# A hybrid attention and SSM layer on one core: the capped decay differences and the first conv tap on ScalarE

## The chip, the cores and the metric

The kernel runs on one core of a Trainium2 chip. The metric is the device time of one execution in microseconds. Before the change it is 1166.08 us, the median of three runs (1162.01, 1166.08 and 1166.91).

## What is computed

One layer of a decoder trunk over 1024 tokens of width 1024, in float32. The input is normalised and modulated, one input projection of 6672 columns feeds a stick-breaking attention group and a Mamba-2 SSM group of 16 heads, and both outputs go through one output projection and a final norm. The change lies in the SSM branch, of which the reference reads, cut to what matters:

```
xbc = silu(causal_depthwise_conv(xbc, conv_w, conv_b))      # 4 taps per channel and a bias
xs, b_ssm, c_ssm = split(xbc)                               # 1024 + 256 + 256 channels
log_decay = dt * a                                          # per token and head
a_cum = cumsum(log_decay within a chunk of 128)             # falls, since a < 0
seg = a_cum[l] - a_cum[s]
decay = exp(where(s <= l, seg, -inf))
y_diag = einsum(cb * decay, xdt)                            # cb = C . B in the chunk
y_off  = einsum(C, state before the chunk, exp(a_cum))
y = y_diag + y_off + x * d_skip
```

The kernel holds a chunk's matrix with s on the partitions and l along the row. It caps seg at 0 before the exponential, so that nothing overflows where s > l, and the mask comes in with cb.

## The kernel before

TensorE does every projection as three float32r matmuls (high x high, low x high, high x low part of both operands), 24 of 128x512 for one tile of 128 columns and half of the tokens (`mm_f`, L265 to L270). A projection tile needs weights loaded by SyncE, a rounded copy `whi` and the rest `wlo` (`split`, L180), and the two PSUM banks of the pool `pj` take turns. Before the pinned part of the program `whi` is made on ScalarE and `wlo` on GpSimd.

The program has three stretches. First the modulation and the first projections, up to about 100 us. Then, to about 360 us, the SSM stretch that the change touches: `conv_tile` (L494) projects one tile of 128 channels, copies it out of PSUM on ScalarE (`conv_in`, L476) into a row `om`, and `conv_post` (L484) does the four taps on VectorE, a Tanh on ScalarE and a last product on VectorE. Twelve tiles go this way: two of C, two of B, eight of x. `ssd_group(g)` (L575) does the scan for eight heads, in eight chunks of 128 tokens. L1003 weaves group 0 with the conv tiles of group 1, L1004 weaves group 1 with four gate tiles (`gate_ssm`) and the first query and key tiles (`qk`). The third stretch, from L1007 (`pinned[0] = True`), is attention with the remaining projections and the output projections, in written program order on every engine.

In the SSM stretch nothing is pinned: the order of each engine's queue is made by a scheduler when the program is built, from its own idea of each instruction's cost. What is issued on an engine runs in that order, and an instruction whose input isn't ready holds all that stand behind it.

A chunk of `ssd_group` runs as follows. ScalarE's queue issues a transfer (L584) that brings the eight heads' a_cum rows, spread to all partitions, into `abc`, half of a tile `be`; the pool has four such tiles, so a chunk's transfer waits until the chunk four before it has let go of its tile. VectorE makes the capped differences `m` in the other half, one 128x128 instruction per head (L585 to L587). ScalarE takes the exponential of `m` and of `abc` (L588, L589). VectorE copies the chunk's last decays to `cdy` (L591). TensorE makes B.C and the transpose of B into `pt` (L594, L595), VectorE copies both out into `cbm` (L597, L598) and multiplies `m` by it (L599). TensorE transposes the x tiles into `pz` (L603), VectorE multiplies by dt into `xd`, a buffer of `v` or `sq` (L605), GpSimd scales `abc` by C (L609). Then come TensorE's sixteen matmuls of the chunk (L614, L619), VectorE's four sums into the x tiles (L622), and the new state: a product on GpSimd (L625), a matmul (L628) and two VectorE instructions into `st` (L634, L635).

All calls on VectorE, ScalarE, GpSimd and SyncE pass through a helper, so the profile gives L62 as their line; they are told apart by the tiles they write and read. `x8` behind a row means eight such instructions in a row.

Of the kernel before, what the change touches and what calls it, by code (L numbers as in the profile page):

```python
# [10 lines left out]
AF = mybir.ActivationFunctionType  # L11
ALU = mybir.AluOpType
# [3 lines left out]
S = 1024  # L16
# [10 lines left out]
def hybrid_layer_kernel(  # L27
# [22 lines left out]
    def K(ins):  # L50

        return tc.keep_in_program_order(ins) if pinned[0] else ins
# [11 lines left out]
    V, A, G, SP = Engine(nc.vector), Engine(nc.scalar), Engine(nc.gpsimd), Engine(nc.sync)  # L64
# [14 lines left out]
    def mk(pool, tag, shape, dtype=F32, bufs=None):  # L79
        uid[0] += 1  # L80
        kw = {} if bufs is None else {"bufs": bufs}
        return pool.tile(shape, dtype, tag=tag, name=f"{tag}_{uid[0]}", **kw)

    def const(name, shape, dtype=F32):
        return cp.tile(shape, dtype, tag=name, name=name)
# [4 lines left out]
    def duo(dtype=F32):  # L90
        return mk(sp, "be", [P, 2, S], dtype, bufs=4)

    def bank(pool, tag):
        return mk(pool, tag, [P, HALF])
# [379 lines left out]
    tri, trigt, acT, dtb, dcol, cw, aneg = late_consts()  # L474
# [4 lines left out]
    def conv_buf():  # L479
        u = mk(sp, "om", [P, 1028], bufs=2)  # L480
        G.memset(u[:, 0:3], 0.0)
        return u

    def conv_post(j, u, dst):  # L484
        V.tensor_scalar(dst, u[:, 3:3 + S], cw[:, 36 + j:37 + j], cw[:, 48 + j:49 + j],
                        op0=ALU.mult, op1=ALU.add)
        for tap in range(2, -1, -1):
            V.scalar_tensor_tensor(dst, u[:, tap:tap + S], cw[:, 12 * tap + j:12 * tap + j + 1],
                                   dst, op0=ALU.mult, op1=ALU.add)
        th = mk(sp, "th", [P, S], bufs=1)  # L490
        A.activation(th, dst, AF.Tanh)
        V.scalar_tensor_tensor(dst, th, 1.0, dst, op0=ALU.add, op1=ALU.mult)

    def conv_tile(j, dst):  # L494
        box = []

        def evac(b, ps):
            if b == 0:
                box.append(conv_buf())
            conv_in(box[0], b, ps)  # L500

        yield from inproj_f(C_XBC + j * P, evac)
        conv_post(j, box[0], dst)
# [9 lines left out]
    for j, ps, dst in ((10, ps_c, Cg[0]), (8, ps_b, Bg[0])):  # L513
        u = conv_buf()
        for b in range(2):
            conv_in(u, b, ps[b])
        conv_post(j, u, dst)
# [47 lines left out]
    acum = const("acum", [P, TB, 16])  # L565
# [9 lines left out]
    def ssd_group(g):  # L575
        Ct, Bt = Cg[g], Bg[g]
        st = None
        hs = slice(8 * g, 8 * g + 8)
        for ch in range(TB):
            ts_ = slice(ch * P, (ch + 1) * P)  # L580
            am = duo().rearrange("p u (h t) -> p u h t", t=P)
            abc, m = am[:, 0], am[:, 1]
            r0 = ch * 16 + 8 * g
            A.dma_start(abc, acT_d[r0:r0 + 8, :].unsqueeze(0).broadcast_to([P, 8, P]))  # L584
            for h in range(8):  # L585
                V.tensor_scalar(m[:, h, :], abc[:, h, :], acum[:, ch, 8 * g + h:8 * g + h + 1], 0.0,
                                op0=ALU.subtract, op1=ALU.min)  # L587
            A.activation(m, m, AF.Exp)  # L588
            A.activation(abc, abc, AF.Exp)  # L589
            cd = mk(sp, "cdy", [P, 8], bufs=2)  # L590
            V.tensor_copy(cd, abc[:, :, P - 1])  # L591

            pc = bank(pt, "pt")
            K(T.matmul(pc[:, 0:P], Bt[:, ts_], Ct[:, ts_], start=True, stop=True))  # L594
            K(T.transpose(pc[:, P:2 * P], Bt[:, ts_], ident))  # L595
            cbm = mk(sp, "cbm", [P, 2, P], bufs=2)
            V.tensor_tensor(cbm[:, 0, :], pc[:, 0:P], tri, op=ALU.mult)  # L597
            V.tensor_copy(cbm[:, 1, :], pc[:, P:2 * P])  # L598
            V.tensor_tensor(m, m, cbm[:, 0:1, :].broadcast_to([P, 8, P]), op=ALU.mult)  # L599

            px = bank(pz, "pz")
            for j in range(4):
                K(T.transpose(px[:, j * P:(j + 1) * P], xs[4 * g + j][:, ts_], ident))  # L603
            xd = mk(sp, "sq" if ch % 2 else "v", [P, 2, 8, 64], bufs=2 if ch % 2 else 3)
            V.tensor_tensor(xd[:, 0], px.rearrange("p (h r) -> p h r", r=64),  # L605
                            dt_t[:, ch, hs].unsqueeze(2).broadcast_to([P, 8, 64]), op=ALU.mult)
            py = bank(pz, "pz")
            if ch > 0:
                G.tensor_tensor(abc, abc, Ct[:, ts_].unsqueeze(1).broadcast_to([P, 8, P]), op=ALU.mult)  # L609
            for j in range(4):  # L610
                for e in range(2):
                    h = 2 * j + e
                    po = py[64 * e:64 * e + 64, j * P:(j + 1) * P]
                    K(T.matmul(po, xd[:, 0, h, :], m[:, h, :], start=True, stop=(ch == 0)))  # L614
                if ch > 0:
                    for e in range(2):
                        h = 2 * j + e
                        po = py[64 * e:64 * e + 64, j * P:(j + 1) * P]
                        K(T.matmul(po, st[:, h, :], abc[:, h, :], start=False, stop=True))  # L619
            for j in range(4):  # L620
                jj = 4 * g + j
                V.scalar_tensor_tensor(xs[jj][:, ts_], xs[jj][:, ts_], dcol[:, jj:jj + 1],  # L622
                                       py[:, j * P:(j + 1) * P], op0=ALU.mult, op1=ALU.add)
            if ch < TB - 1:
                G.tensor_tensor(xd[:, 1], xd[:, 0],  # L625
                                dte[:, ch, hs].unsqueeze(2).broadcast_to([P, 8, 64]), op=ALU.mult)
                pst = bank(pv, "pv")
                K(T.matmul(pst, cbm[:, 1, :], xd[:, 1].rearrange("p h r -> p (h r)"), start=True, stop=True))  # L628
                nst = mk(sp, "st", [P, 8, 64], bufs=2)
                psv = pst.rearrange("p (h r) -> p h r", r=64)  # L630
                if ch == 0:
                    V.tensor_copy(nst, psv)
                else:
                    V.tensor_tensor(nst, st, cd.unsqueeze(2).broadcast_to([P, 8, 64]), op=ALU.mult)  # L634
                    V.tensor_tensor(nst, nst, psv, op=ALU.add)  # L635
                st = nst
            yield 3.4
# [363 lines left out]
    pieces += [("y", i, g, y_d) for i in range(TB) for g in range(2)]  # L1001

    weave((ssd_group(0), 27.0), (chain(bc_tiles(1), xs_tiles(range(4, 8))), 62.0))  # L1003
    weave((ssd_group(1), 27.0), (chain(*[gate_ssm(j) for j in range(4)], qk(0, box)), 63.0))  # L1004
    load_upto(2)
    ahead(), ahead()
# [117 lines left out]
    for i in range(TB):  # L1124
# [27 lines left out]
        for n, (c0, c1) in enumerate(cuts):  # L1152
            ps = bank(pj, "pj")
            for k in range(KT):
                yh, yl = yt[k // 4]
                ks = slice(k % 4 * P, (k % 4 + 1) * P)
                for m, (y, w) in enumerate(((yh, wa_h[k]), (yh, wa_l[k]), (yl, wa_h[k]))):
# [5 lines left out]
                                   op0=ALU.mult, op1=ALU.mult)  # L1163
# [42 lines left out]
```

## Time and profile before

| | |
|---|---|
| median of three runs | 1166.08 us |
| profiled execution, its own time | 1164.38 us |
| its span, first to last instruction | 1162.5 us |
| mean granted TensorE clock | 0.981 of full |
| TensorE busy | 1091.7 us, 94% |
| VectorE busy | 791.7 us, 68% |
| ScalarE busy | 445.6 us, 38% |
| GpSimd busy | 354.7 us, 31% |

A row of a group gives the engine, the operation, what it writes and reads by tile name, the shapes, the count, the busy time in us and the mean of one in ns, and the idle time just before it with what ended it. A row of the waits reads "engine line waited for: us in total, times, longest". Matmuls are pipelined: each is shown longer than the distance to the next one, so the distance of their starts tells the rate.

### The profile page before, as it was taken

To read this page: it belongs to the slowest core of one execution; us is meant where nothing else is said; L and a number is where in the kernel's file an instruction comes from. 1 tells how busy PE (TensorE), PEld (TensorE's weight loads), DVE (VectorE), ACT (ScalarE), POOL (GpSimd) and SP (SyncE) were. 2 spreads that over 40 slices of the span, in tenths; PEclk is the share of its full clock that TensorE was granted. 3 is DMA by queue.
4 is the path that set the end of the run, shared out by engine and by line. 5 is a ranking of instruction groups with operands and counts; after the bars stand their busy time and mean duration, and the time that the engine had idled before them with its cause. 6 is when DMAs were issued, how large, how long until landed. Compare 5 with 4: busy or idle time off the path is not lost. (4 is left out here: it accounts for less than half of the span.)

```text
span 1162.5 us, 16503 instructions
## 1 busy us (share of the span) xinstructions
PE 1091.7 (94%) x6401; PEld 854.3 (73%) x6401; DVE 791.7 (68%) x1292; ACT 445.6 (38%) x942; POOL 354.7 (31%) x245
## 2 busy tenths in 40 slices
PE   5999999898999988999999999999999979999997
PEld 4688877676787766778767787677787747778886
DVE  4566989998975854572697845967549678673444
ACT  4432423332222442444444645445545434350101
POOL 2322445435672343120221202212122134344220
PEclk9999999998999999999999999999999979999999
DMA  9802422122221121110231102111011413375331
GB/s 292 219 20 55 120 55 82 55 73 75 89 66 35 55 73 55 28 55 10 74 91 56 54 19 65 55 28 56 19 37 50 163 42 104 106 259 184 130 133 73
DMA packets 101473, 96.16 MB, mean 83 GB/s; under 512 B 5670, under 2 KB 87826, under 8 KB 101396
## 3 DMA queue, kind: packets, MB, share of 16 engines
q1 hardware_dynamic: 98724, 86.61, 24.7%
q10 hardware_dynamic: 2448, 8.46, 2.2%
q8 instruction: 50, 0.82, 0.3%
q14 instruction: 27, 0.22, 0.1%
q0 software_dynamic: 224, 0.06, 0.0%
HBM read 78.26 MB, written 16.84 MB: 82 GB/s over the span
## 5 line engine op out<-in xcount | busy, mean ns | idle before, releaser
L62 POOL TENSOR_TENSOR wlo<-raw,whi 128x512 fp32r<-128x512 f32 (+1 forms) x113 | 164.2, 1455 | 404.7 <-DVE whi L62 200.0
L269 PE MATMUL pj<-hh,whi 128*128 128x512 f32 x576 | 242.5, 421 | 12.8 <-DVE be L62 5.7
L269 PE MATMUL pj<-hl,whi 128*128 128x512 f32 x576 | 229.7, 399 | 0.0
L269 PE MATMUL pj<-hh,wlo 128*128 128x512 f32 x576 | 229.2, 398 | 0.0
L62 ACT COPY be<-pt 128x512 f32<-128x512 f32 (+3 forms) x190 | 91.2, 480 | 181.2 <-PE pt L823 180.5
L269 PEld LDWEIGHTS pj<-hh,whi 128*128 128x128 f32 x576 | 109.8, 191 | 43.1 <-DVE be L62 7.0
L269 PEld LDWEIGHTS pj<-hh,wlo 128*128 128x128 f32 x576 | 109.5, 190 | 26.3 <-issue 1.0
L269 PEld LDWEIGHTS pj<-hl,whi 128*128 128x128 f32 x576 | 110.0, 191 | 19.5 <-issue 1.1
L823 PE MATMUL pt<-ident,be 128*128 128x128 f32 x569 | 97.7, 281 | 12.8 <-ACT be L62 12.3
L823 PEld LDWEIGHTS pt<-ident,be 128*128 128x128 f32 x569 | 68.2, 142 | 47.9 <-ACT be L62 36.4
L62 DVE TENSOR_TENSOR_SCAN om<-om,ident 128x128 f32<-128x128 f32 x64 | 40.7, 637 | 88.9 <-ACT om L62 88.9
L62 ACT ACTIVATE be<-pz 128x512 f32<-128x512 f32 (+3 forms) x192 | 100.5, 524 | 0.0
L62 DVE TENSOR_TENSOR_SCAN bc<-bc 128x896 f32<-128x896 f32 (+6 forms) x56 | 85.3, 1523 | 2.0
L62 DVE TENSOR_TENSOR_SCAN om<-om 128x896 f32<-128x896 f32 (+6 forms) x56 | 78.4, 1401 | 2.0
L62 ACT ACTIVATE om<-pz 128x512 f32<-128x512 f32 (+2 forms) x96 | 47.6, 495 | 78.8 <-PE pz L768 77.4
L62 POOL TENSOR_TENSOR sq<-sq,th 128x512 f32<-128x512 f32 (+1 forms) x18 | 36.4, 2021 | 114.6 <-ACT th L62 114.6
L835 PE MATMUL pv<-be,v 128*64 128x256 f32 (+1 forms) x640 | 70.4, 365 | 0.0
L311 PE MATMUL pj<-whi,hh 128*128 128x256 f32 (+1 forms) x224 | 67.1, 300 | 0.9 <-ACT om L62 0.9
L768 PE MATMUL pz<-big,big 64*128 64x384 f32 (+2 forms) x576 | 65.2, 357 | 0.2 <-DVE big L62 0.2
L835 PEld LDWEIGHTS pv<-be,v 128*64 128x64 f32 x640 | 43.5, 137 | 29.6 <-issue 9.3
L313 PE MATMUL pj<-whi,hl 128*128 128x256 f32 (+1 forms) x224 | 64.0, 286 | 0.0
L312 PE MATMUL pj<-wlo,hh 128*128 128x256 f32 (+1 forms) x224 | 63.9, 285 | 0.0
(276 smaller groups left out, 2165.4 us busy)
## 6 DMA issues: line engine op xcount, KB each, us to landing
raw<-in_w_in_dram SPq DMA_DIRECT2D x102, 256.0 KB, 2.9
be<-acT_d ACTq DMA_DIRECT2D x16, 512.0 KB, 3.7
big<-in_x_dram SPq DMA_DIRECT2D x11, 512.0 KB, 6.0
aw<-in_w_ada_dram SPq DMA_DIRECT2D x16, 256.0 KB, 5.4
u_d<-big SPq DMA_DIRECT2D x8, 512.0 KB, 3.4
y_d<-bc SPq DMA_DIRECT2D x8, 512.0 KB, 2.6
raw<-in_w_ada_dram SPq DMA_DIRECT2D x16, 256.0 KB, 2.7
raw<-u_d SPq DMA_DIRECT2D x16, 256.0 KB, 3.0
```

The costliest lines, as they stand in the source:

```text
L62: return lambda *args, **kw: K(op(*args, **kw))
L269: K(T.matmul(ps, w[:, ws], h[:, b * HALF:(b + 1) * HALF], start=(k == 0 and n == 0), stop=(k == KT - 1 and n == 2)))
L311: K(T.matmul(ps[:, :n], h_hi[k][:, ts_], whi[:, ws], start=(k == 0), stop=False))
L312: K(T.matmul(ps[:, :n], h_hi[k][:, ts_], wlo[:, ws], start=False, stop=False))
L313: K(T.matmul(ps[:, :n], h_lo[k][:, ts_], whi[:, ws], start=False, stop=(k == KT - 1)))
L768: K(T.matmul(zs[e][:, :mw], a[r, i * P:(i + 1) * P], k_[r, c0:c0 + mw], start=(n == 0), stop=(n == 2)))
L823: K(T.transpose(ptt[:, (j - j0) * P:(j - j0 + 1) * P], be[:, j * P:(j + 1) * P], ident))
L835: K(T.matmul(pav[p][64 * e:64 * e + 64, (q0 + u) * P:(q0 + 2) * P], vs[p][:, j * P + 64 * e:j * P + 64 * e + 64], tl[e][:, u:2, j * P:(j + ...
```

## The change

The first conv tap with the bias goes from a VectorE instruction to a ScalarE ACTIVATE (Identity, with a scale and a bias per partition). The capped difference min(abc - acum, 0) is written as -max(acum - abc, 0): eight ScalarE ACTIVATEs per chunk (Relu, scale -1, acum as bias) give the positive value, and the exponential behind them takes scale -1.

```
 def conv_post(j, u, dst):
-    V.tensor_scalar(dst, u[:, 3:3 + S], cw[:, 36 + j:37 + j], cw[:, 48 + j:49 + j],
-                    op0=ALU.mult, op1=ALU.add)
+    A.activation(dst, u[:, 3:3 + S], AF.Identity, scale=cw[:, 36 + j:37 + j], bias=cw[:, 48 + j:49 + j])
...
         for h in range(8):
-            V.tensor_scalar(m[:, h, :], abc[:, h, :], acum[:, ch, 8 * g + h:8 * g + h + 1], 0.0,
-                            op0=ALU.subtract, op1=ALU.min)
-        A.activation(m, m, AF.Exp)
+            A.activation(m[:, h, :], abc[:, h, :], AF.Relu, scale=-1.0,
+                         bias=acum[:, ch, 8 * g + h:8 * g + h + 1])
+        A.activation(m, m, AF.Exp, scale=-1.0)
```

That is 12 + 128 instructions. Since the scheduler orders the stretch anew, the queues change around them as well. Two places are shown; numbers behind a name tell its buffers apart in the program.

VectorE, group 0, the end of its chunk 3 (counted from 0), before. `v_1724` is the product xd of chunk 4, `big_1585` an x tile of group 1 in its conv taps, `be_1924` the tile of chunk 6, and the four rows with `dcol` are the sums of chunk 3:

```order
L62 TENSOR_SCALAR be_1924<-be_1924,acum 128x128 x8
L62 COPY cdy_1821<-be_1809 128x8
L62 TENSOR_SCALAR big_1585<-om_1679,cw 128x1024
L62 SCALAR_TENSOR_TENSOR big_1585<-om_1679,cw,big_1585 128x1024 x2
L62 SCALAR_TENSOR_TENSOR big_982<-big_982,dcol,pz_1633 128x128
L62 SCALAR_TENSOR_TENSOR big_1056<-big_1056,dcol,pz_1633 128x128
L62 SCALAR_TENSOR_TENSOR big_1130<-big_1130,dcol,pz_1633 128x128
L62 SCALAR_TENSOR_TENSOR big_1204<-big_1204,dcol,pz_1633 128x128
L62 SCALAR_TENSOR_TENSOR big_1585<-om_1679,cw,big_1585 128x1024
L62 TENSOR_TENSOR st_1658<-st_1658,pv_1656 128x512
L62 TENSOR_TENSOR v_1724<-pz_1719,dt_t 128x512
```

The same place on VectorE in the changed program:

```order
L62 COPY cdy_1821<-be_1809 128x8
L62 SCALAR_TENSOR_TENSOR big_1585<-th_1768,big_1585 128x1024
L62 SCALAR_TENSOR_TENSOR big_982<-big_982,dcol,pz_1633 128x128
L62 SCALAR_TENSOR_TENSOR big_1056<-big_1056,dcol,pz_1633 128x128
L62 SCALAR_TENSOR_TENSOR big_1130<-big_1130,dcol,pz_1633 128x128
L62 SCALAR_TENSOR_TENSOR big_1204<-big_1204,dcol,pz_1633 128x128
L62 TENSOR_TENSOR st_1658<-st_1658,pv_1656 128x512
L62 TENSOR_TENSOR v_1724<-pz_1719,dt_t 128x512
```

The nine TENSOR_SCALAR are gone, the taps of `big_1585` have moved ahead of this place, and its last product, which needs ScalarE's Tanh `th_1768`, has moved up to stand before the sums.

ScalarE, group 0, from the transfer of chunk 7 (`be_2020`) to that of the next chunk, before. `om` and `pj` are a projection tile being copied out, `whi` and `raw` weights:

```order
L62 DMA be_2020<-acT_d 128x1024
L62 COPY om_1865<-pj_1784 128x512
L62 ACTIVATE th_1768<-big_1585 128x1024
L62 CAST whi_2086<-raw_2082 128x512
L62 ACTIVATE be_2020<-be_2020 128x1024 x2
L62 CAST whi_2090<-raw_2084 128x512
L62 COPY om_1865<-pj_1868 128x512
L62 DMA be_2155<-acT_d 128x1024
```

The same stretch of ScalarE's queue in the changed program:

```order
L62 DMA be_2020<-acT_d 128x1024
L62 ACTIVATE be_2020<-be_2020,acum 128x128 x8
L62 CAST whi_2090<-raw_2084 128x512
L62 COPY om_1865<-pj_1868 128x512
L62 ACTIVATE be_2020<-be_2020 128x1024 x2
L62 ACTIVATE big_1771<-om_1865,cw 128x1024
L62 DMA be_2155<-acT_d 128x1024
```

The eight Relus stand right behind the transfer that they read, a copy out of `pj` behind them, and the first tap of the next conv tile behind the exponentials.

## The prediction

> **What bounds the kernel now.** I read the page first, then the windows of 50 us, then who waited for whom in the stretch that the change touches. The page says that TensorE is the engine that fills the span:
>
> ```profile
> PE 1091.7 (94%) x6401; PEld 854.3 (73%) x6401; DVE 791.7 (68%) x1292; ACT 445.6 (38%) x942; POOL 354.7 (31%) x245
> ```
>
> The profiled execution took 1164.38 us with a span of 1162.5 us, so 1.9 us lie around it; the median of the three runs is 1166.08 us, 1.7 us above it. The sum below is made as a difference against the profiled execution and then taken from the median.
>
> The changed lines run between about 100 and 360 us, while the chunks of the SSM scan are woven into projections. The third column below is TensorE's busy time, then weight loads, VectorE, ScalarE and GpSimd; after them the granted clock.
>
> ```profile
> 200.00:250.00 50.00, 42.45 (x266) 33.74 (x265) 49.82 (x86) 14.73 (x20) 20.28 (x13) 0.93 0.21 63
> 250.00:300.00 50.00, 44.77 (x244) 34.46 (x243) 43.30 (x78) 17.10 (x23) 25.74 (x15) 0.93 0.27 85
> 300.00:350.00 50.00, 47.42 (x298) 37.45 (x297) 41.57 (x70) 12.08 (x17) 33.34 (x18) 0.97 0.24 74
> ```
>
> ```profile
> 100.00:360.00 260.00, 240.54 (x1379) 189.31 (x1377) 227.51 (x391) 79.91 (x109) 123.64 (x74) 0.97 0.25 74
> ```
>
> VectorE is busy 49.8 of 50 us in the worst of them and 227.5 of 260 in all; ScalarE only 79.9 of 260. TensorE idles 260 - 240.5 = 19.5 us. Its waits there, in the view of waits (total, times, longest), say for whom:
>
> ```profile
> PE pz L614 <- DVE v L62: 5.9, 4, 2.5
> PE pz L603 <- DVE big L62: 3.8, 3, 3.4
> PE pz L614 <- DVE sq L62: 2.9, 2, 2.6
> PE pt L594 <- DVE cbm L62: 2.7, 2, 1.7
> PE pj L269 <- DVE th L62: 2.1, 1, 2.1
> PE pj L269 <- ACT om L62: 1.6, 1, 1.6
> PE pv L628 <- POOL sq L62: 0.4, 1, 0.4
> ```
>
> They add up to 19.4 us, 17.4 of them behind VectorE. So in this stage, and not in the rest of the kernel, VectorE's queue sets the pace.
>
> A wait costs more than itself, because the matmuls after it run slowly for a while:
>
> ```profile
> 319.67 0.72 PE L269 MATMUL pj<-hh,whi 128*128 128x512 f32 x1 [2.14 <-DVE th L62]
> 320.19 0.63 PE L269 MATMUL pj<-hl,whi 128*128 128x512 f32 x1
> ...
> 323.30 0.39 PE L269 MATMUL pj<-hh,whi 128*128 128x512 f32 x1
> 323.53 0.39 PE L269 MATMUL pj<-hl,whi 128*128 128x512 f32 x1
> ```
>
> At full clock one projection matmul follows another after 0.23 us; after the wait of 2.14 us the first spacing is 0.52. The granted clock of the three windows gives the size: 50 x (0.07 + 0.07 + 0.03) = 8.5 us. All that this stage could give back is therefore 19.4 + 8.5 = 28 us. The Trainium skill (TensorE: Matmul & The Clock Gate, Part 1: The HAM clock gate) puts the drop after at least one idle window of about 3.4 us; the trace shows it after 2.14 us, so the measurement decides. By the page alone only the one wait of 3.4 us would cost clock, nearly all of the clock term below would fall out, and the time would be about 1155 us.
>
> **What the change takes from VectorE.** 128 capped differences and the first taps (twelve in all, eight of them in the second row):
>
> ```profile
> L62 DVE TENSOR_SCALAR be<-be,acum 128x128 f32<-128x128 f32 x128 | 46.2, 427 | 2.9 <-DMA be<-acT_d 2.9
> ...
> L62 DVE TENSOR_SCALAR big<-om,cw 128x1024 f32<-128x1024 f32 x8 | 7.4, 928 | 2.7 <-ACT om L62 2.6
> ```
>
> ```profile
> L62 DVE TENSOR_SCALAR be<-be,acum x128: 270/274/2447, 121.9 to 318.7; 128x128 f32<-128x128 f32 x128
> ```
>
> That is 46.2 + 7.4 = 53.6 us. The median of 274 ns against a mean of 427 says that some of it is waiting inside the instruction, which may move to its neighbours: 128 x 0.274 + 7.4 = 42.5 us is the lower bound. VectorE falls from 227.5 to between 174 and 185 us of 260, 67 to 71%.
>
> How this reaches TensorE is seen at one wait. VectorE's time line (start, length), and TensorE's:
>
> ```profile
> 194.94 3.46 DVE L62 TENSOR_SCALAR be<-be,acum 128x128 f32<-128x128 f32 x8
> ...
> 198.40 0.80 DVE L62 TENSOR_SCALAR big<-om,cw 128x1024 f32<-128x1024 f32 x1
> ...
> 206.62 0.68 DVE L62 TENSOR_TENSOR v<-pz,dt_t 128x512 f32<-128x512 f32 x1
> ```
>
> ```profile
> 207.36 0.69 PE L614 MATMUL pz<-be,v 128*64 128x128 f32 x4 [2.55 <-DVE v L62]
> ```
>
> The 128x512 product at 206.62 is what TensorE waits for; 3.46 + 0.80 = 4.3 us of removed instructions stand ahead of it in a queue without gaps, and in the new order they are gone from there. The wait of 2.55 us goes. What is late next at this place is the tap that needs the Tanh, which now comes from a busier ScalarE.
>
> **What it adds to ScalarE.** No such instruction is in the trace, so nearest rows:
>
> ```profile
> L62 ACT ACTIVATE be<-be 128x1024 f32<-128x1024 f32 x32 | 32.3, 1052 | 72.4 <-DVE be L62 72.4
> ...
> L62 ACT ACTIVATE om<-pz 128x512 f32<-128x512 f32 x32 | 19.2, 600 | 68.3 <-PE pz L768 68.2
> ...
> L62 ACT ACTIVATE be<-pz,shc,gsc 128x512 f32<-128x512 f32 x8 | 6.2, 774 | 10.9 <-DVE gsc L62 6.0 <-PE pz L412 4.9
> ...
> L62 ACT ACTIVATE st<-st 128x128 f32<-128x128 f32 x1 | 0.3, 310 | 0.8 <-DVE st L62 0.8
> ```
>
> ```profile
> 123.61 2.01 ACT L62 ACTIVATE be<-be 128x1024 f32<-128x1024 f32 x2 [4.17 <-DVE be L62]
> ```
>
> A 128x128 ACTIVATE takes 0.310 us; a per-partition operand adds (0.774 - 0.600)/2 = 0.087; so one Relu is 0.40 us alone. Two in a row overlap by 2 x 1.052 - 2.01 = 0.09, which leaves 0.30 each: eight take 2.5 us, 128 take 39 to 51. I take the 39, as they stand in runs of eight. A first tap is 1.052 + 0.174 = 1.23 us, eight 9.8. ScalarE rises from 79.9 to 129 to 141 us of 260, about half. It has the room; the two Exps stay, and the sign that the first now applies is a constant of the instruction and costs nothing. The taps run before 100 us meet no wait of TensorE and count nothing; without that cover two of them would cost 2.5 us.
>
> **Where ScalarE can become late.** Its queue is in order, and what now stands behind the Relus is the copying out of projection tiles, the Tanhs and weight casts. The Relus wait for their transfer:
>
> ```profile
> DMA to landing us min/median/max: 1.6/3.7/7.7
> ```
>
> From issue of a chunk's transfer: 3.7 landing + 2.5 Relus + 2.0 Exps + 0.6 for the copy behind them (the 0.600 row) = 8.8 us until a projection bank is free. Two banks take turns, so TensorE needs it after 24 matmuls of the other one, 5.5 us, and a chunk's own matmuls:
>
> ```profile
> L269 PE MATMUL pj<-hh,whi 128*128 128x512 f32 x248 | 101.3, 409 | 3.8 <-DVE th L62 2.1 <-ACT om L62 1.6
> ```
>
> Three such kinds x 248 x 0.23 = 171 of the 240.5 us; the rest over 16 chunks is 4.3 us each. So the room is 9.8 us against a lag of 8.8: enough at the median landing, 3.0 us short at the longest one. Twelve transfers wait for a buffer (the first four find theirs free). I take four of them at a landing halfway up, 5.7 us, short by 1.0: 4 us of new waits, with bounds of 0 and 12 x 3.0 = 36.
>
> **The sum.** Of the 17.4 us behind VectorE I take 14 as recovered and leave 3.4 at the start of the second group, where the longest wait hangs on the last conv tile: its chain gets 0.4 us longer (1.23 for 0.8), and its Tanh stands behind a transfer and eight Relus. The 1.6 and 0.4 us stay. The clock comes back in proportion, 8.5 x 14/19.4 = 6 us. Gain 14 + 6 - 4 = 16 us: the profiled execution goes to 1148, the median to 1150. After the stage the order is the written one and TensorE works through it; nothing there waits for a clock time, so the gain is kept.
>
> **The rivals.** *Everything comes back:* no new wait, 28 us, 1138 us. For it speaks ScalarE at half load; against it the chain of the last conv tile. Chance 0.10.
>
> *VectorE stays the pace:* waits inside its instructions move to the neighbours, and half of the 17.4 us stays: 8.7 + 3.8 - 4 = 8.5 us, 1157.5. For it speaks the 274 against 427 ns. Chance 0.10.
>
> *ScalarE's lag takes it back:* a mean landing of 6.2 us makes each of twelve chunks 1.5 us short, 18 us against 20 recovered: 1164. Against it stands the median of 3.7. Chance 0.14.
>
> *ScalarE becomes the pace, slower:* projection tiles are copied out late in every chunk. At the longest landing 12 x 3.0 = 36 us against 20: 1182. It decides from a shortage of 1.7 us per chunk, a landing of 6.4 us; over 0.5% slower needs 2.2. One Relu costs 0.40 us where VectorE's costs 0.27, which speaks for it; the 50 to 54% load speaks against. Chance 0.08. The Trainium skill (ScalarE: Activation LUTs, Rules for kernel authors) gives relu, max, min, add and mul to VectorE and not to ScalarE; by that rule this change is in the wrong direction and this rival would be the likely one. The trace agrees on the price of one instruction, but its 227.5 against 79.9 us of busy time decides here for the other side.
>
> My forecast keeps 0.58. The range reaches to 1140, where it takes in half of the first rival, and to 1164 with the third; outside stay the slower one and the rest of the first, about 0.13, and the tail of the third. About 0.5%, 5.8 us, is what a measurement of this kernel can tell from no change. Faster by more: 0.58 + 0.10 + 0.10 = 0.78; within: 0.14; slower: 0.08.
>
> **What would show it.** In the profile after: VectorE at 174 to 185 us between 100 and 360, ScalarE at 129 to 141, Relus of 0.3 to 0.4 us; TensorE's idle time in the stage 6 to 10 us instead of 19.5, its waits for v, sq and cbm gone, the clock of these windows at 0.98 or more, and the first scores about 16 us earlier. I am wrong if TensorE waits for the copies of ScalarE (om, th) by more than 10 us, if ScalarE idles for the be transfers by more than 3 us a chunk, or if the waits behind VectorE keep more than 8 us.

## The result and the profile after

The changed kernel takes 1135.28 us (median of four runs, 1131.97 to 1137.06), the kernel before 1165.22 on the same chip: a ratio of 0.974, with a 95% interval of 0.971 to 0.978. The forecast was 1150, the range 1140 to 1164: the time fell below it. What happened is the rival "everything comes back", which had a chance of 0.10. The profiled span fell by 27.2 us, from 1162.5 to 1135.3; the medians lie 29.9 apart, and the sums below are of the span. All times are of executions in the usual state of the clock; one of the kernel with two more copies on ScalarE, 1762.94 us at a granted clock of 0.56, was in a slow one and is left out.

The page of the kernel after, its first row. VectorE lost 54.6 us (791.7 before), ScalarE gained 50.9:

```profile
PE 1083.9 (95%) x6401; PEld 849.0 (75%) x6401; DVE 737.1 (65%) x1152; ACT 496.5 (44%) x1082; POOL 354.2 (31%) x245
```

The SSM stage is taken here from 100 us to TensorE's first scores matmul. That one starts at 359.3 us before and at 332.3 after, so nearly the whole gain lies ahead of it. The windows of that stage (length, then busy time of TensorE, weight loads, VectorE, ScalarE and GpSimd, granted clock), first of the kernel before:

```profile
100.00:359.30 259.30, 239.84 (x1375) 188.85 (x1373) 227.50 (x390) 79.32 (x108) 123.64 (x74) 0.97 0.25 74
```

and of the kernel after, the whole stage and the two windows that were the worst ones:

```profile
100.00:332.30 232.30, 230.97 (x1377) 182.93 (x1375) 173.67 (x253) 128.65 (x247) 124.12 (x75) 1.00 0.27 82
200.00:250.00 50.00, 49.14 (x316) 39.22 (x315) 41.46 (x62) 35.42 (x70) 24.63 (x15) 1.00 0.26 75
250.00:300.00 50.00, 50.00 (x325) 38.49 (x324) 39.70 (x65) 25.81 (x53) 38.60 (x22) 1.00 0.33 106
```

TensorE's idle time fell from 259.3 - 239.8 = 19.5 us to 1.3, and the same matmuls took 8.9 us less, because the clock is 1.00 instead of 0.97. 18.1 + 8.9 = 27.0 us.

The clock's part came in whole stretches. In the trace before it was at half for five times 3.41 us inside the stage, from 207.13, 234.44, 268.57 (two in a row) and 319.77 us, which is 5 x 3.41 / 2 = 8.5 us of the 8.9. The first of them with the same length behind it, and then the 3.4 us after a wait of 2.62 us, which had none; the granted clock is the third number from the end:

```profile
207.13:210.54 3.41, 3.18 (x30) 3.19 (x32) 3.41 (x9) 0.63 (x2) 2.26 (x2) 0.50 0.00 0
210.54:213.95 3.41, 3.41 (x20) 2.40 (x17) 3.41 (x7) 2.82 (x4) 0.22 (x1) 1.00 0.69 208
222.70:226.10 3.40, 3.40 (x39) 2.70 (x40) 3.40 (x12) 0.46 (x1) 1.42 (x1) 1.00 0.02 5
```

VectorE stands at 173.7 us in the stage, the end of the predicted range at which all waiting inside the removed instructions vanishes with them, and ScalarE at 128.7, the end at which the Relus overlap. TensorE's waits in this stage after the change, all of them:

```profile
PE pj L269 <- DVE th L62: 0.9, 1, 0.9
PE pt L593 <- DVE cbm L62: 0.5, 1, 0.5
```

Before there were 17.4 us behind VectorE, 1.6 behind ScalarE's `om` and 0.4 behind GpSimd. ScalarE's new rows:

```profile
L62 ACT ACTIVATE be<-be,acum 128x128 f32<-128x128 f32 x128 | 39.5, 390 | 30.8 <-DMA be<-acT_d 30.8
...
L62 ACT ACTIVATE big<-om,cw 128x1024 f32<-128x1024 f32 x8 | 9.9, 1240 | 0.1
```

One Relu takes 390 ns, 128 take 39.5 us (39 predicted), the eight taps 9.9 (9.8 predicted). ScalarE waits 30.8 us for transfers, and TensorE lost no more than 0.9 us by it.

### The profile page after: what moved, and what is told of

Read it like the earlier page. It is cut to its first block, busy times and chain, and to the rows that moved or that the text cites. A ratio compares the mean times of both kernels' runs of the same rounds, so it can differ in the third digit from the quotient of the medians.

```text
span 1135.3 us, 16484 instructions
## 1 busy us (share of the span) xinstructions
PE 1083.9 (95%) x6401; PEld 849.0 (75%) x6401; DVE 737.1 (65%) x1152; ACT 496.5 (44%) x1082; POOL 354.2 (31%) x245
```

## The experiments

Four theories were open. **A:** the change takes load off VectorE, and nothing else counts. **B:** the chain counts: the exponential no longer waits for VectorE (72.4 us of ScalarE's idle time before). **C:** the new order of the queues happens to be a better one. **D:** ScalarE's lag is a real price that this order escapes narrowly. Every kernel was timed beside the kernel before. "Stage" is the length from 100 us to the first scores, "VectorE" its busy time there. The runs with a load on ScalarE, with the transfers moved, and a load that fell outside the stage are not in the table; they have their figures below.

| kernel | VectorE | stage | ratio to before, 95% |
|---|---|---|---|
| changed kernel | 173.7 | 232.3 | 0.974 [0.971, 0.978] |
| the same once more | 174.1 | 232.2 | 0.975 [0.972, 0.978] |
| two more copies on ScalarE | 175.1 | 237.9 | 0.977 [0.973, 0.982] |
| 16 row maxima a chunk added | 192.5 | 241.3 | 0.985 [0.983, 0.986] |
| Relus only | 195.5 | 237.6 | 0.979 [0.978, 0.980] |
| 6 dummies a chunk added | 205.7 | 242.0 | 0.984 [0.980, 0.988] |
| taps only | 216.8 | 251.1 | 0.993 [0.991, 0.996] |
| before | 227.5 | 259.3 | 1 |
| 16 dummies behind the copies | 257.3 | 282.4 | 1.018 [1.015, 1.020] |
| 16 dummies a chunk added | 259.7 | 280.8 | 1.018 [1.016, 1.020] |

### Each half alone

The changed kernel with the first tap put back on VectorE:

```
-    A.activation(dst, u[:, 3:3 + S], AF.Identity, scale=cw[:, 36 + j:37 + j], bias=cw[:, 48 + j:49 + j])
+    V.tensor_scalar(dst, u[:, 3:3 + S], cw[:, 36 + j:37 + j], cw[:, 48 + j:49 + j], op0=ALU.mult, op1=ALU.add)
```

> Only the 128 capped differences go to ScalarE; the first conv taps stay on VectorE. Theory A (VectorE's load in the stage sets the pace, and each us taken off it comes back in proportion, with the slow clock behind each wait): 46 of the 55.8 us go, so 46/55.8 of the 30 us are gained, 25 us, about 1140. Theory B (what counts is that the exponential no longer waits for VectorE, a chain inside one engine): all of it is gained here, about 1135. Theory C (the scheduler's new order does it, not the load): no fixed number, the gain need not follow the share.

The changed kernel with the capped differences put back on VectorE, and the exponential without its sign:

```
-            A.activation(m[:, h, :], abc[:, h, :], AF.Relu, scale=-1.0, bias=acum[:, ch, 8 * g + h:8 * g + h + 1])
-        A.activation(m, m, AF.Exp, scale=-1.0)
+            V.tensor_scalar(m[:, h, :], abc[:, h, :], acum[:, ch, 8 * g + h:8 * g + h + 1], 0.0, op0=ALU.subtract, op1=ALU.min)
+        A.activation(m, m, AF.Exp)
```

> Only the twelve first conv taps go to ScalarE; the capped differences stay on VectorE. Theory A: 9.6 of 55.8 us go, 5 us are gained, about 1160. Theory B: nothing, about 1165; or up to 3 us lost, since each conv tile's chain gets 0.4 us longer. Theory C: no fixed number.

The Relus alone give 2.1%, the taps alone 0.7%. Together that is 2.8% against 2.5% measured for both. With the taps alone the differences stay on VectorE, the exponential still waits 59.9 us for it (72.4 before), and the stage is 8.2 us shorter. That speaks against B as the only cause but does not settle it, since the wait fell as well; the next runs do.

### VectorE loaded again, ScalarE left as it is

The changed kernel with sixteen dummy operations on VectorE per chunk, each of the form that was removed, a quarter as wide; `spare` is a tile that nobody reads:

```
+            for n in range(16):
+                V.tensor_scalar(spare, ident[:, 0:32], acum[:, ch, 8 * g + n % 8:8 * g + n % 8 + 1], 0.0, op0=ALU.subtract, op1=ALU.min)
```

> The changed kernel with VectorE's load given back: per chunk 16 TENSOR_SCALAR of 128x32 on constants, results used by nobody, some 0.13 to 0.2 us each, 33 to 50 us in all. Theory A: VectorE is again at 90% and more in the stage, TensorE waits for v, sq, cbm and big come back, 1155 to 1165. Theory B: the exponentials still don't wait for VectorE, so 1135 to 1140. Theory C: the order is new once more, no fixed number; if the time stays at 1135 with VectorE's load back, load was not the cause.

It takes 1183.17 us, slower than before, though the exponential does not wait for VectorE, as in the changed kernel. TensorE's waits in its stage:

```profile
PE pt L597 <- DVE cbm L62: 10.8, 4, 3.5
PE pz L617 <- DVE v L62: 9.1, 3, 3.9
PE pz L617 <- DVE sq L62: 5.0, 2, 3.0
PE pz L617 <- DVE be L62: 4.1, 2, 3.7
PE pj L269 <- DVE th L62: 3.2, 2, 2.8
PE pz L606 <- DVE big L62: 2.2, 1, 2.2
PE pv L631 <- POOL v L62: 0.6, 1, 0.6
```

They are those of the kernel before in their kind, and larger: v, sq, cbm, big and th, with be in addition, all but 0.6 us behind VectorE. The same with six dummies instead of sixteen:

> The changed kernel with VectorE's load given back to about the size that was taken: 6 TENSOR_SCALAR of 128x32 per chunk on constants, 96 at the 0.476 us that 256 of them took in the run before, 46 us; their results are used by nobody. Theory A (VectorE's busy time from 100 us to the first scores sets how long that stretch is: 174 us gave 232, 195 gave 238, 217 gave 251, 227 gave 259, 260 gave 281): 174 + 46 = 220 us, a stretch of about 253, 21 us longer than the changed kernel's, about 1153 to 1157. Theory B (the gain is that the exponential does not wait for VectorE any more): as the changed kernel, 1132 to 1137.

The six cost 37.7 us of busy time instead of 46, so VectorE had 206 us in the stage and not 220. The scheduler also put all 96 of them between 114 and 177 us, so they load the first third of the stage and not each chunk. The time of 1145.09 is below the expectation, and the table has it where 206 us stand. What the two runs show together: load on VectorE alone brings the waits and the time back, the more of it the more. Theory B falls.

### ScalarE loaded

The changed kernel with each Relu done twice, and three times, for the same result:

```
-        for h in range(8):
+        for h in list(range(8)) * 2:
```

> The changed kernel with each Relu done twice (the same values): 39 us more on ScalarE, 2.5 us more between a chunk's transfer and whatever stands behind. Theory A with the room formula (9.8 us of room for a copy out of a projection bank; lags of 5.7 to 8.1 us measured in the changed kernel, one of 10.3): most lags stay at or under 10.6, a few are 0.5 to 1 us too long, so 1135 to 1142. Rival (ScalarE is already near its limit, as its 31 us of waiting for the transfers would suggest): 12 chunks each 2.5 us later, 30 us, about 1165.

> The changed kernel with each Relu done three times (the same values): 77 us more on ScalarE than the change gave it, some 206 of the 240 us. The second set cost 8 to 12 us. Room formula (a copy may stand 9.8 us behind a chunk's transfer; lags now some 5 us above the changed kernel's 6 to 8): each of twelve chunks 2 to 2.5 us short, 25 to 30 us over the second set, about 1170. Rival (only ScalarE's busy share counts, as VectorE's does): 206 of 240 is 86%, at which VectorE cost some 19 us over the floor, about 1152.

They take 1143.90 us (ratio 0.985, interval 0.984 to 0.987) and 1149.39 (0.988, 0.984 to 0.991), with ScalarE at 166 of 241.6 and at 201 of 249.0 us of the stage. The formula of the prediction, with its room of 9.8 us, would have the last one near 1170. TensorE's waits with the Relus done three times:

```profile
PE pz L602 <- DVE big L62: 8.7, 2, 8.2
PE pz L613 <- DVE v L62: 1.6, 2, 0.8
PE pj L269 <- ACT om L62: 0.9, 2, 0.6
PE pv L627 <- POOL v L62: 0.6, 1, 0.6
```

The copies of ScalarE are never more than 0.6 us late. ScalarE's time line of the kernel with three times the Relus says why:

```profile
208.84 0.99 ACT L62 ACTIVATE be<-be,acum 128x128 f32<-128x128 f32 x3
209.73 0.57 ACT L62 COPY om<-pj 128x512 f32<-128x512 f32 x1
210.20 1.29 ACT L62 ACTIVATE be<-be,acum 128x128 f32<-128x128 f32 x4
```

The copy stands in the middle of a run of Relus: the scheduler puts it where the bank is needed. What becomes late is one place, the wait of 8.2 us up to 262.10 us, where TensorE turns over the x tiles for the first time in group 1. ScalarE's time line just before it:

```profile
252.26 3.33 ACT L62 ACTIVATE be<-be,acum 128x128 f32<-128x128 f32 x11
255.47 1.15 ACT L62 CAST whi<-raw 128x512 fp32r<-128x512 f32 x2
256.50 3.34 ACT L62 ACTIVATE be<-be,acum 128x128 f32<-128x128 f32 x11
259.72 1.06 ACT L62 ACTIVATE th<-big 128x1024 f32<-128x1024 f32 x1
```

The Tanh of the last conv tile stands behind 22 Relus. VectorE's last tap, which the Tanh reads, ends at 255.52, so two casts and the second eleven hold it for 4.2 us, half of the wait; VectorE's last product and the matmul follow it at once. D holds for that place with three times the Relus, and not for the copies. With the Relus done twice TensorE idles 8.1 us in the stage, in waits of 2.0 us at most, 0.4 of them for ScalarE's copies; what makes the others longer was not traced. So load on ScalarE has a price too, although ScalarE is far from full: nothing else counts, as A has it, is too strong.

### The transfers moved to SyncE

The changed kernel with the spread transfers issued by SyncE, so that ScalarE's queue holds no transfer:

```
-            A.dma_start(abc, ...)
+            SP.dma_start(abc, ...)
```

> The changed kernel with the sixteen spread transfers issued from SyncE's queue instead of ScalarE's. Theory A: ScalarE's 31 us of waiting for them are slack and TensorE has 1.3 us of waits left in the stage, so no difference, within 3 us of the changed kernel. Rival (the waiting on ScalarE still costs): up to 10 us faster. A transfer on SyncE can also be held behind weight loads there: slower by up to 10 us.

It takes 1142.67 us (0.983, 0.979 to 0.986), 0.8% slower than the changed kernel on the same chip (1133.65 us, below). TensorE's idle time in the stage is 6.8 us in place of 1.3. SyncE's queue waits in the stage as a whole, the first row of it:

```profile
SPq L62 <- POOL wlo L62: 145.1, 30, 13.6
```

The weight loads in that queue wait for buffers, by up to 13.6 us at a time, and now the transfers stand behind them. ScalarE then waits for transfers 38.3 us in place of 30.8, with 8.1 at the longest in place of 4.9.

### The same again, and further

The changed kernel was run once more, beside the loads:

> The changed kernel again, for comparison on the same chip as the three others: 0.974 of the kernel before, about 1132 to 1136.

1133.65 us; the result repeats. Then the changed kernel with two more operations taken to ScalarE:

```
-            V.tensor_copy(cd, abc[:, :, P - 1])
+            A.copy(cd, abc[:, :, P - 1])
...
-            V.tensor_copy(cbm[:, 1, :], pc[:, P:2 * P])
+            A.copy(cbm[:, 1, :], pc[:, P:2 * P])
```

> The changed kernel with two more small operations a chunk taken from VectorE to ScalarE: the copy that spreads the decays out of PSUM (cdy) and the second of the two copies of the C and B rows (cbm). If VectorE's load is all that the change bought (theory A), the SSM stage already stands on TensorE's own work of about 231 us, so VectorE's busy time falls below 174 us and nothing comes of it: stage 231 to 232 us, 1133 to 1136 us in all. If there were still something to gain behind VectorE, the stage would fall below 230 us and the kernel below 1131 us. If ScalarE's queue is by now the one that answers late (the lag theory), TensorE waits over 5 us for ScalarE's copies and the time is 1140 us or more.

The median is 1137.26 us: no gain, and the stage got 5.6 us longer. Of TensorE's 6.3 us of waits there 2.7 are now behind ScalarE, 1.5 for the moved copy into `cbm` and 1.2 for `om`, and the rest behind VectorE. 32 instructions left VectorE, and its busy time in the stage is 175.1 us against 173.7. The taps in the changed kernel, and then in this one:

```profile
L62 DVE SCALAR_TENSOR_TENSOR big<-om,cw,big 128x1024 f32<-128x1024 f32 x24 | 37.2, 1551 | 8.4 <-ACT big L62 8.0
```

```profile
L62 DVE SCALAR_TENSOR_TENSOR big<-om,cw,big 128x1024 f32<-128x1024 f32 x24 | 44.8, 1870 | 11.9 <-ACT big L62 11.6
```

Here the waiting inside instructions did move to the neighbours, as the rival "VectorE stays the pace" had it for the change itself. The first scores came 5.6 us later, and the span is the same 1135.2 us as the changed kernel's 1135.3, because the stretch after them was shorter in this run; why was not settled. By the medians the two lie 2 us apart, and the intervals of their ratios overlap. No version was found that beats the change.

### What the long instructions wait for

The removed differences had a median of 274 ns and a mean of 427. The dummies of the first load run show it more strongly, so two runs put the question with them. The first try had its sixteen operations a chunk read a constant:

```
+            for n in range(16):
+                V.tensor_reduce(spare[:, n:n + 1], ident[:, 0:32], axis=AX.X, op=ALU.max)
```

> The changed kernel with sixteen dummy operations a chunk on VectorE again, as in the load run that took 1183 us, but each a row maximum of one 128x32 tile (one tensor in, one column out) in place of the operation of a tensor with a scalar column. That run's dummies had a median of 242 ns and a mean of 476 ns. If the difference was waiting for something that VectorE and GpSimd share, and which the row maximum does not need, mean and median now lie within 15% of one another, the 256 dummies take some 50 to 60 us, VectorE stands near 225 to 235 us, the stage near 255 to 262 us by the curve of the other runs, and the kernel takes about 1157 to 1165 us. If the waiting belongs to any VectorE operation at that place, the mean stays near twice the median and the time near 1183 us.

It told nothing: the scheduler put all 256 ahead of 54 us, outside the stage, and the time was 1137.50 us. The second try reads `cbm`, so that they run in their chunk, once as a row maximum and once in the form of the removed instructions:

```
+            for n in range(16):
+                V.tensor_reduce(spare[:, n:n + 1], cbm[:, n % 2, 0:32], axis=AX.X, op=ALU.max)
```

```
+            for n in range(16):
+                V.tensor_scalar(spare, cbm[:, n % 2, 0:32], acum[:, ch, 8 * g + n % 8:8 * g + n % 8 + 1], 0.0, op0=ALU.subtract, op1=ALU.min)
```

> In the run before, the sixteen row maxima a chunk read a constant, and the program's order put all 256 of them ahead of 54 us, outside the SSM stage; it says nothing on the question. Here they read cbm, which VectorE has just copied, so they must run in the stage, sixteen a chunk behind the copies. If the long means of VectorE's small operations are waiting for something shared with GpSimd that a row maximum does not need, their mean lies within 15% of their median of some 170 to 180 ns, they take some 45 us and VectorE has about 220 us in the stage; by the curve of VectorE's load the stage is then about 252 to 256 us, the kernel about 1156 to 1160 us. If the waiting meets any VectorE operation, the mean is 1.5 times the median or more, 65 us or more, VectorE stands at 240 us or more and the kernel at about 1167 us or more.

> The same place, input and count as the row maxima, but each dummy a 128x32 difference and minimum with a scalar column, the form of the removed instructions. By the theory of something shared with GpSimd the median is about 240 ns and the mean 1.5 to 2 times that, as in the load run that took 1183 us: 95 to 125 us, VectorE at 255 us or more in the stage, stage 275 us or more, the kernel at 1175 to 1190 us. If the long means came from where those dummies stood (ahead of the copies, behind a wait), mean and median agree here too, the dummies take some 62 us, VectorE stands near 237 us, the stage near 266 us and the kernel near 1168 us.

The row maxima take 1144.43 us, the differences 1183.28. The tile row of the row maxima (count, then shortest, median and longest in ns), and then that of the differences:

```profile
L62 DVE TENSOR_REDUCE spare<-cbm x256: 167/176/189, 130.6 to 329.5; 128x1 f32<-128x32 f32 x128
```

```profile
L62 DVE TENSOR_SCALAR spare<-cbm,acum x256: 226/242/2385, 130.6 to 379.6; 128x32 f32<-128x32 f32 x128
```

No row maximum took longer than 189 ns; among the differences the longest took 2385, and the mean is 480. Same place, same input, same count, and one form waits while the other does not. For what, VectorE's and GpSimd's time lines of that last kernel say:

```profile
143.72 4.34 DVE L62 TENSOR_SCALAR spare<-cbm,acum 128x32 f32<-128x32 f32 x5
...
149.17 1.28 DVE L62 TENSOR_SCALAR spare<-cbm,acum 128x32 f32<-128x32 f32 x1
```

```profile
143.84 2.37 POOL L62 TENSOR_TENSOR be<-be,bc 128x1024 f32<-128x1024 f32 x1 [3.69 <-DVE cdy L62]
146.18 1.30 POOL L62 TENSOR_TENSOR wlo<-raw,whi 128x512 fp32r<-128x512 f32 x1
148.90 1.50 POOL L62 TENSOR_TENSOR wlo<-raw,whi 128x512 fp32r<-128x512 f32 x1 [1.43 <-ACT whi L62]
```

Five dummies of 0.24 us fill 4.34 us, and GpSimd's two operations at that place take 3.67 together; the single dummy of 1.28 us ends at 150.45, GpSimd's operation at 150.40. It is the same all through the trace: 49 of the 256 dummies took over 0.31 us, and every one of them ended 0.04 us after an operation of GpSimd did. Not one dummy ran wholly inside such an operation; of the row maxima 145 ran wholly inside one, and none of them took longer than 189 ns. In the kernel before, 19 of the 128 removed differences were long, and each ended 0.08 us after an operation of GpSimd. Such an instruction of VectorE waits until GpSimd's is done. The Trainium skill (SBUF — State Buffer, SBUF: two separate sides) states this, for some forms of VectorE's operations, as an exclusive lock on a shared pair of ports, held for a whole instruction; these runs agree. Here the dummies have 122.8 us of busy time where 256 x 0.242 = 62 would do.

The row maxima missed their expectation in size: placed back to back they overlap, 25.2 us in all and not 45, so VectorE had 192.5 us. With 241.3 us of stage they lie above the Relus alone, which had 195.5 and 237.6. So the table is a curve only to within about 6 us below 210 us, where the kernel with the transfers on SyncE lies 7 us off as well (171.6 us of VectorE's work, a stage of 239.3); above that, the order of the loads is the order of the stages but for two neighbours that lie 1.6 us apart.

## Why the prediction was wrong, point by point

**What bounds the stage: right.** VectorE's queue set the pace there. From 217 us of load upwards each further us on VectorE costs about 0.7 us of stage: (280.8 - 251.1) / (259.7 - 216.8). At the changed kernel's 174 us nothing is left to gain in its order, since TensorE's own work at full clock is 231 of 232.3 us. What is left to C are the 6 us by which the table departs from a curve: every kernel of it has its own order, and the load sorts them.

**What leaves VectorE and what ScalarE pays: right.** 39.5 and 9.9 us on ScalarE, against 39 and 9.8. Of VectorE the upper end came true, since the waiting went with the instructions; the lower end, 42.5 us, was too careful here.

**The step that failed: "new waits 4", by the landing of 5.7 us.** I put four of the twelve waiting transfers halfway up to the longest landing, 7.7 us. That longest one was not theirs to have: it belongs to the first four transfers, which are issued within 1.3 us of one another and which I had set apart myself. In the kernel before, the first four, and then the twelve:

```profile
DMA to landing us min/median/max: 6.3/7.0/7.7
DMA to landing us min/median/max: 3.3/3.7/4.7
```

The profile has the landing of only some of the twelve, seven before and eight after; in the changed kernel they have 3.3, 4.0 and 4.9. At 4.7 the lag of the prediction, 8.8 us at a landing of 3.7, is 9.8 us, just the room, so its own formula gives no new wait worth counting, while the bound of 36 us and both rivals built on longer landings rest on none that these transfers showed.

The lag itself was also set too long for many chunks. I put both exponentials, 2.0 us, between the transfer and the copy out of the bank. In the changed order the copy stands in front of them in five of the twelve chunks, where it ends 6.2 to 7.9 us after the transfer's issue; the second piece of ScalarE's order, shown ahead of the prediction, has exactly that, a cast and a copy and then the two exponentials. In three more a copy runs even ahead of the Relus. The Relus wait for their transfer 30.8 / 12 = 2.6 us a chunk. One chunk of the changed kernel shows the long case, ScalarE's time line first:

```profile
237.56 0.33 ACTq L62 DMA_DIRECT2D be<-acT_d  x1
242.46 2.46 ACT L62 ACTIVATE be<-be,acum 128x128 f32<-128x128 f32 x8 [3.72 <-DMA be<-acT_d]
244.96 1.06 ACT L62 ACTIVATE th<-big 128x1024 f32<-128x1024 f32 x1
245.93 1.99 ACT L62 ACTIVATE be<-be 128x1024 f32<-128x1024 f32 x2
247.82 0.57 ACT L62 ACTIVATE th<-pj 128x512 f32<-128x512 f32 x1
```

From issue at 237.56 to the end of ScalarE's read of the bank at 248.39 are 10.8 us, over the room of 9.8 that I had worked out. The landing took 4.9 us, and a Tanh that the formula did not have stands in between. This is a gate tile, whose bank VectorE reads as well, right after ScalarE and until 249.41. TensorE's next matmul in that bank has the one sizeable wait that is left:

```profile
249.46 0.50 PE L269 MATMUL pj<-hh,whi 128*128 128x512 f32 x1 [0.86 <-DVE th L62]
```

So TensorE waited for it once and not four times, and the price was 0.9 us in place of 4. The same mistake carried the rivals "ScalarE's lag takes it back" and "ScalarE becomes the pace", 0.22 together: even with the Relus done three times the kernel is still 1.2% faster than before, though with two it has already given back over a third of the gain (ratio 0.985 against 0.974).

**"I take 14 as recovered" of the 17.4: too low.** I left 3.4 us at the start of the second group. Nothing waits there in the changed kernel; with the Relus done three times that wait is back, 8.2 us long. And the 1.6 and 0.4 us that I let stand went too; that they followed from VectorE's delays is likely, but no run shows it apart. 18.1 us came back, 4.1 more than the sum had.

**The clock, "6 us" in proportion: too low, 8.9.** Taken in proportion to idle time it went with the term above. It does not go in proportion here: it is lost in stretches of 3.41 us at half the clock, 1.7 us each, and with no wait over 0.9 us left all five vanish. The three errors are 4 + 4.1 + 2.9 = 11.0 us, the difference between the 16 forecast and the 27.0 measured in the stage.

**The range and the chances.** None of the signs that I named for being wrong came: no wait of TensorE for ScalarE's copies, 2.6 us a chunk for transfers against 3, waits behind VectorE of 1.4 us against 8. I had looked for errors on the slow side alone. With VectorE at 174 of some 235 us, and ScalarE at 55%, the plain reading was that the queue which made all waits is no longer full; that was the rival with 0.10, and should have been the forecast or near it.

**The rule against moving such work to ScalarE.** One Relu does cost more than what it replaces, 390 ns against the median of 274. Against the mean of 427, which counts the waiting beside GpSimd, it costs less. The Trainium skill (Perfetto Trace Analysis, Optimizing Scalar/DVE Operations) says that where VectorE is saturated, taking work to ScalarE may make sense. At 49.8 of 50 us it was, and these runs agree with that sentence.

## What to carry to other kernels

Where one engine's queue makes nearly all waits of the engine that bounds a stage, take load off it until the bound engine's own work is the stage's length, and start the forecast from "all waits and the clock come back"; subtract only for a new wait that the new order shows instruction by instruction, and take the cost in it, here a landing, from the cases that stand as it does and not from the spread of all. Count an instruction of VectorE that waits for GpSimd at its mean in this place, not at its median: what it waits for inside belongs to its price, and a move to ScalarE can save that too. At the floor the one further move that was tried brought nothing, and waiting went to the neighbours.

## What the runs showed of the hardware that was not expected

VectorE's difference with a scalar column waits for GpSimd's whole operation, by up to 2.1 us for a 0.24 us instruction, while a row maximum at the same place never does. Two-input operations of VectorE, the taps, went from 37.2 to 44.8 us with the same work when two copies a chunk had left the queue. They wait for GpSimd too: the long ones, 8 of 24 in the changed kernel and 10 of 24 here, each end 1.08 us after one of its operations ends, and a tap that waits for nothing takes 1.27. Why more of them met one stayed open.

TensorE's clock after the change is 1.00 in the stage where no wait exceeds 0.9 us, 0.97 before. Slow stretches came with waits of 2.07, 2.14, 2.55 and 3.43 us there, and none with one of 2.62, so a wait's length alone does not decide it. In this stage the slower matmuls cost 8.9 us beside the 18.1 of the waits.
